# Elementwise steps of three token mixers moved from GpSimd to VectorE in a two-layer hybrid decoder step

## The chip, the cores and the metric

The kernel runs on one core of a Trainium2 chip. The metric is the device time of one execution of the whole program, in microseconds. A core has TensorE (PE: matmuls and transposes; PEld is its weight load), VectorE (DVE), ScalarE (ACT), GpSimd (POOL) and SyncE (SP, which issues the DMAs here). Each engine runs its own queue of instructions in the order in which the program gives them, and engines wait for each other by semaphores.

## What is computed

Two trunk layers over 1104 tokens (16 learned meta tokens, 1024 prompt tokens, 8 sequences of 8 decode tokens). In each layer three mixers read one input projection: a gated delta rule (4 heads, key and value width 128), a Mamba2 scan (4 heads of 64, state 128) and sliding-window attention with rotary positions. Their outputs are joined and projected, and a SwiGLU block follows.

```
(dn_qkv, dn_z, dn_b, dn_a, ssm_xbc, ssm_z, ssm_dt, sw_q, sw_k, sw_v) = split_cols(h @ lw['w_in'], IN_WIDTHS)
a_mat = where(strict, beta_i * (k_i . k_j) * decay_ij, 0);  attn = (q_i . k_j) * decay_ij     # delta rule
o_c = q_dec @ s + attn @ v_new;  s = s * g_last + k_dec^T v_new
attn = (c_i . b_j) * decay_ij;  y_intra = attn @ (x * dt);  h = h * g_last + xdt^T b_dec       # scan
rope(x) = [x1*cos - x2*sin, x2*cos + x1*sin]                                                  # attention
x = x + rmsnorm(mixed @ w_out);  x = x + rmsnorm((silu(gate) * up) @ w_ffn_out)
```

## The kernel before

Matmuls of weights run in pairs of half-precision values (a high and a low part, three products each); the small matmuls of the mixers run in fp32. Tokens are cut into nine tiles, eight of 128 and one of 80 (the 64 decode tokens and the last 16 of the prompt), and the delta rule works on quads of tiles (4, 4, 1) per head.

The program is not written in its final order. Every step is a generator (`dense`, `swa_in`, `ssm_pre`, `ssm_seq`, `dn_inv`, `dn_prep`, `dn_chain` and others), and class `Plan` picks, again and again, the first generator by priority whose data is ready on the planner's own clock of TensorE. For that it keeps a clock per engine: an elementwise instruction of n elements per partition is costed at `RATE[engine][0] * n + RATE[engine][1]` ns.

```
RATE = {"V": (1.04, 90.0), "S": (0.85, 55.0), "G": (2.1, 60.0)}
```

V is VectorE, S ScalarE, G GpSimd; the power function on GpSimd has a surcharge. So the engine that an instruction is given to alters the order of everything around it, on all engines. `conv_post` (the convolutions, tiles `u` and `R`) and the weight splitting (`wsp`) add VectorE work when the planner's VectorE clock is free.

The steps that the change touches, with their lines:
- `rope_tile` (660): per token tile four products of the projected q and k (`qkv`) with sines and cosines into `rp`, and one sum. It runs right after each of the first nine projections of a layer.
- `lt_make` (1482) and `ssm_pre` (1847): per tile of the scan, the decay matrix `lt` times the causal mask, and x times three scalings (`xdt`, `xde`, `xD`). VectorE then multiplies `lt` with a product of TensorE, and TensorE reads `lt`, `xdt` and `xde`.
- `dn_inv` (1543) and `dn_prep` (1651): per quad the decay matrix `M` times the mask and times beta; per tile `qe` (in `prep`) times q.
- `dn_chain` (1683), for a head's last tile: spread values `ye` and the eight decode states `Sb` times their decay. VectorE writes `r` and `S` of the chain; `ps_ch` is the one PSUM bank of the chain.
- `ssm_seq` (1897), last tile: `xe` and the decode states `hs`, as in `dn_chain`.

GpSimd also computes every inverse square root (`rsqrt`, line 572: `rqy`, one multiply-add and one power), diagonals (`affine_select`), fills, and small copies (`coll`). All engine calls go through one wrapper, so every instruction's line is L215, and rows are told apart by tiles.

Of the kernel before, what the change touches and what calls it, by code (L numbers as in the profile page):

```python
# [284 lines left out]
def build(tc, A, depth=DEPTH):  # L285
# [3 lines left out]
    V, S, G, T, DQ = (P.engine(e, k) for e, k in ((nc.vector, "V"), (nc.scalar, "S"), (nc.gpsimd, "G"),  # L289
                                                 (nc.tensor, "T"), (nc.sync, "D")))  # L290
# [26 lines left out]
    MUL, ADD, SUB, MAX = ALU.mult, ALU.add, ALU.subtract, ALU.max  # L317
# [342 lines left out]
    def rope_tile(qkv, i, C, L):  # L660
        cs, sn = (L.KSW(n)[:C, i * 64:i * 64 + 64] for n in ("cs", "sn"))
        x = qkv[:C, :384].rearrange("p (h e d) -> p h e d", e=2, d=32)
        t1, t2 = (abp.tile([128, 6, 2, 32], F32, tag="a", name="rp")[:C] for _ in range(2))
        snv = sn.rearrange("p (e d) -> p e d", e=2)
        csv = cs.rearrange("p (e d) -> p e d", e=2)
        for e in range(2):
            G.tensor_tensor(t2[:, :, e, :], x[:, :, 1 - e, :],
                            snv[:, e:e + 1, :].to_broadcast([C, 6, 32]), op=MUL)
            G.tensor_tensor(t1[:, :, e, :], x[:, :, e, :],
                            csv[:, e:e + 1, :].to_broadcast([C, 6, 32]), op=MUL)  # L670
        G.tensor_tensor(qkv[:C, :384], t1.rearrange("p h e d -> p (h e d)"),
                        t2.rearrange("p h e d -> p (h e d)"), op=ADD)

    def put_mixed(mx, c0, n, ps, p0=0, pn=128, view=None):
# [807 lines left out]
    def lt_make(lt, p, L, ths, C):  # L1482

        n = len(ths)
        for k, (i, h) in enumerate(ths):
            act(lt[:, k], p[:C, k, :C], AF.Relu, bias=L.gc[:C, i, h:h + 1], scale=-1.0)
        act(lt, lt, AF.Exp, scale=-1.0)
        mk = U[:, None, :] if C == 128 else U8[:80, None, :]
        G.tensor_tensor(lt, lt, mk.to_broadcast([C, n, C]), op=MUL)


    QUADS = ((0, 1, 2, 3), (4, 5, 6, 7), (8,))
# [2 lines left out]
    def col(X, i):  # L1495
        return X["c"] if i == 8 else X["u"][:, i * 128:i * 128 + 128]
# [46 lines left out]
    def dn_inv(L, w, it):  # L1543
# [6 lines left out]
        for h, b in it:  # L1550
            H = L.HS[h]
            C, n = tsz(b[0]), len(b)
            yield (("gates", l),)
            yield "inv"
            p = v4(PS("inv"))
            for k, i in enumerate(b):
                T.transpose(p[:, k, :C], gc[:C, i, h:h + 1].to_broadcast([C, 128]), ident[:C, :C])
            M = t4("M")[:C, :n, :C]
# [2 lines left out]
            yield None  # L1561
            act(M, M, AF.Exp, scale=-1.0)
            mk = U[:, None, :] if C == 128 else U8[:80, None, :]
            G.tensor_tensor(M, M, mk.to_broadcast([C, n, C]), op=MUL)
            yield None
            yield (("q", l, h), ("k", l, h))
            G.tensor_tensor(M, M, H["b2"][:C, b[0]:b[0] + n].unsqueeze(2).to_broadcast([C, n, C]), op=MUL)
            yield None
            yield lambda: outst[0] < 3
            outst[0] += 1  # L1570
# [80 lines left out]
    def dn_prep(L):  # L1651

        l, gc = L.l, L.gc
        for h in range(4):
            H = L.HS[h]
            for b in PAIRS:
                C, n = tsz(b[0]), len(b)
                yield (("q", l, h), ("k", l, h), ("v", l, h), ("sk", l, h), ("gates", l))
                yield lambda: outst[1] < 2
                outst[1] += 1  # L1660
                X = big([128, 4, 2, 128], F32, "prep")
                qe, kd, vt = X[:, 0], X[:, 1], X[:, 2]
                yield "tr"
                p = v4(PS("tr"))
                for k, i in enumerate(b):
                    T.transpose(p[:, k, :C], gc[:C, i, h:h + 1].to_broadcast([C, 128]), ident[:C, :C])
                act(qe[:, :n, :C], p[:, :n, :C], AF.Exp)
                for k, i in enumerate(b):
                    G.tensor_tensor(qe[:, k, :C], qe[:, k, :C], col(H["q"], i), op=MUL)
                yield NOW  # L1670
                yield "tr"
                p = v4(PS("tr"))
                for k, i in enumerate(b):
                    T.transpose(p[:C, k, :], col(H["k"], i), ident)
                    T.transpose(p[:C, 2 + k, :], col(H["v"], i), ident)
                for k, i in enumerate(b):
                    act(kd[:C, k], p[:C, k], scale=H["d2"][:C, i:i + 1])
                    act(vt[:C, k], p[:C, 2 + k], scale=H["sk"][:C, i:i + 1])
                    H["X"][i] = (qe[:, k], kd[:, k], vt[:, k])
                mark(("prep", l, h, b[0]))  # L1680
                yield None

    def dn_chain(L):
# [3 lines left out]
        nE, gl, gls = L.nE, L.gl, L.gls  # L1687
        for h in range(4):
            H = L.HS[h]
            Sst = dnp.tile([128, 128], F32, tag="S", bufs=2, name="S")  # L1690
            V.memset(Sst, 0.0)
            for qd, b in enumerate(QUADS):
                og = None
                C = tsz(b[0])
                for k, i in enumerate(b):
# [3 lines left out]
                    qe, kd, vt = H["X"].pop(i)  # L1699
                    if i == 5:  # L1700
                        Sb = big([128, 8, 128], F32, "Sb")
                        dma(Sb, A["Sb"][l, h])
                    if C != 128:
                        kq = big([128, 8, 128], F32, "kq")
                        G.memset(kq, 0.0)
                        for src, o in ((H["k"]["c"][:, 0:64], 0), (qe[:, 0:64], 64)):
                            d = bass.AP(kq.tensor, kq.offset + o, [list(kq.ap[0]), [136, 8], [1, 8]])
# [58 lines left out]
                if C != 128:  # L1766
                    mark(("S", l, h))
                    later(("S", l, h), lambda h=h, Sst=Sst: dma(A["dn_p"][l, h], Sst))
                    ye = big([128, 4, 128], F32, "ye")
                    for q in range(2):  # L1770
                        o = slice(q * 32, q * 32 + 32)
                        G.tensor_tensor(ye[o], y[o].unsqueeze(1).to_broadcast([32, 4, 128]),
                                        SEGM[o, 4 * q:4 * q + 4].unsqueeze(2).to_broadcast([32, 4, 128]), op=MUL)
                    G.tensor_tensor(Sb, Sb, gls[:, 0:8, h:h + 1].to_broadcast([128, 8, 128]), op=MUL)
                    P.add(1, dn_last(L, h, Sb, ye, kd))

    def dn_last(L, h, Sb, ye, kd):
# [69 lines left out]
    def ssm_pre(L, it):  # L1847
# [6 lines left out]
        for i in it:  # L1854
            C = tsz(i)
# [14 lines left out]
            act(xk[:C], px[:C])  # L1870
            x4 = xk[:C, 0:256].rearrange("p (h d) -> p h d", h=4)
            xdt, xde, xD = r2("xdt", 2), r2("xde", 3), r2("xD", 3)
            G.tensor_tensor(xdt[:C], x4, L.dt[:C, i, :].unsqueeze(2).to_broadcast([C, 4, 64]), op=MUL)
            G.tensor_tensor(xde[:C], x4, L.xdd[:C, i, :].unsqueeze(2).to_broadcast([C, 4, 64]), op=MUL)
            G.tensor_tensor(xD[:C], x4, vec[:C, 20:24].unsqueeze(2).to_broadcast([C, 4, 64]), op=MUL)
            zt = r2("zt", 3)
            yield ((("zt", l, i), "st"),)
            dma(zt[:C].rearrange("p h d -> p (h d)"), zd[l, i * 128:i * 128 + C, :])
# [18 lines left out]
    def ssm_seq(L):  # L1897
# [10 lines left out]
        for i in range(NT):  # L1908
            C = tsz(i)
# [56 lines left out]
            if i == 8:  # L1966
                mark(("hT", l))
                later(("hT", l), lambda: dma(A["ssm_p"][l], h2))
                for g in range(2):
                    xe = big([128, 4, 128], F32, "xe")  # L1970
                    for q in range(2):
                        o = slice(q * 32, q * 32 + 32)
                        G.tensor_tensor(xe[o], xde[o, 2 * g:2 * g + 2].rearrange("p h d -> p (h d)").unsqueeze(1)
                                        .to_broadcast([32, 4, 128]),
                                        SEGM[o, 4 * q:4 * q + 4].unsqueeze(2).to_broadcast([32, 4, 128]), op=MUL)
                    for r_ in range(2):
                        hv = hs[g][:, :, r_ * 64:r_ * 64 + 64]
                        G.tensor_tensor(hv, hv, gls[:, 0:8, 4 + 2 * g + r_:5 + 2 * g + r_]
                                        .to_broadcast([128, 8, 64]), op=MUL)
                    yield None  # L1980
                    pq = []
# [308 lines left out]
```

## Time and profile before

| | us |
|---|---|
| median of 3 runs (2830.35 to 2835.38) | 2833.14 |
| the profiled execution | 2830.23 |
| its span, first to last instruction | 2828.4 |
| TensorE busy | 2719.1 |
| VectorE busy | 2011.9 |
| GpSimd busy | 494.7 |

The profile comes from one execution. Stages follow each other in time in each layer: projections and attention, the scan, the delta rule, the output projection, SwiGLU. TensorE's projections for a later stage fill the time of an earlier one, so a stage is read from the trace by the tiles that are worked on: in the first layer the rotations lie at 35 to 112 us, the scan at 225 to 320 us and the delta rule at 320 to 665 us; in the second at 1440 to 1500, 1627 to 1721 and 1721 to 2066 us.

### The profile page before, as it was taken

To read this page: it belongs to the slowest core of one execution; us is meant where nothing else is said; L and a number is where in the kernel's file an instruction comes from. 1 tells how busy PE (TensorE), PEld (TensorE's weight loads), DVE (VectorE), ACT (ScalarE), POOL (GpSimd) and SP (SyncE) were. 2 spreads that over 40 slices of the span, in tenths; PEclk is the share of its full clock that TensorE was granted. 3 is DMA by queue.
4 is the path that set the end of the run, shared out by engine and by line. 5 is a ranking of instruction groups with operands and counts; after the bars stand their busy time and mean duration, and the time that the engine had idled before them with its cause. 6 is when DMAs were issued, how large, how long until landed. Compare 5 with 4: busy or idle time off the path is not lost. (4 is left out here: it accounts for less than half of the span.)

```text
span 2828.4 us, 49806 instructions
## 1 busy us (share of the span) xinstructions
PE 2719.1 (96%) x19662; PEld 1900.6 (67%) x19662; DVE 2011.9 (71%) x3992; ACT 1281.4 (45%) x3015; POOL 494.7 (17%) x746
## 2 busy tenths in 40 slices
PE   7999998999899999999999989999998999999998
PEld 4767676765688888744458666777646888886443
DVE  6467667655867777868875776676569677777778
ACT  5445456654433333433544455556544333334343
POOL 3205423312200000000260063233122000000002
PEclk9999999999999999999999999999999999999999
DMA  5011100132311111342340111001232111113424
GB/s 196 29 64 47 49 31 32 39 105 92 111 39 52 60 46 57 102 119 97 124 151 19 66 49 42 29 32 52 93 113 89 46 60 47 61 53 105 117 100 150
DMA packets 74092, 209.78 MB, mean 74 GB/s; under 512 B 13361, under 2 KB 24817, under 8 KB 73825
## 3 DMA queue, kind: packets, MB, share of 16 engines
q1 hardware_dynamic: 73856, 206.59, 22.1%
q8 instruction: 154, 2.52, 0.4%
q14 instruction: 82, 0.66, 0.1%
HBM read 175.49 MB, written 33.04 MB: 74 GB/s over the span
## 5 line engine op out<-in xcount | busy, mean ns | idle before, releaser
L215 PEld LDWEIGHTS <-wsp 128*128 128x128 f16 x10704 | 1041.7, 98 | 304.7 <-issue 13.6
L215 PE MATMUL pd<-xn,wsp 128*128 128x336 f16 (+3 forms) x4512 | 737.0, 311 | 2.3 <-DVE m L215 2.1
L215 ACT ACTIVATE wsp<-raw 128x512 f16<-128x512 f32 (+2 forms) x390 | 286.5, 751 | 398.9 <-DVE raw L215 70.6
L215 DVE SCALAR_TENSOR_TENSOR wsp<-raw,wsp 128x512 f16<-128x512 f32 (+2 forms) x390 | 326.8, 848 | 66.2 <-ACT wsp L215 63.4
L215 PEld LDWEIGHTS <-hsp 128*128 128x128 f16 x1848 | 181.0, 98 | 222.0 <-DVE hsp L215 3.5
L215 POOL TENSOR_SCALAR rqy<-ss 128x1 f32<-128x1 f32 (+1 forms) x72 | 69.6, 967 | 1445.6 <-ACT jk L215 1235.4
L215 PE MATMUL pd<-wsp,hsp 128*128 128x512 f16 x924 | 224.1, 381 | 3.4 <-DVE hsp L215 1.7
L215 PE MATMUL ps_o<-wsp,hsp 128*128 128x512 f16 x924 | 222.4, 379 | 0.1
L215 PE MATMUL pd<-wsp,mixed 128*128 128x512 f16 (+1 forms) x864 | 210.3, 381 | 0.0
L215 DVE SCALAR_TENSOR_TENSOR u<-R,lp_cw,u 128x512 f32<-128x512 f32 x216 | 179.6, 866 | 11.3 <-ACT u L215 10.4
L215 ACT ACTIVATE hsp<-hid 128x512 f16<-128x512 f32 x154 | 89.7, 619 | 183.0 <-PE ps_o L215 157.6
L215 PE MATMUL ps_o<-xn,wsp 128*128 128x256 f16 (+1 forms) x1296 | 161.3, 281 | 0.0
L215 PE MATMUL pd<-wsp,xn 128*128 128x512 f16 (+3 forms) x864 | 156.2, 332 | 3.2 <-ACT wsp L215 1.7
L215 PE MATMUL ps_inv<-xn,wsp 128*128 128x256 f16 (+1 forms) x1248 | 154.1, 281 | 0.0
L215 PEld LDWEIGHTS <-mixed 128*128 128x128 f16 (+1 forms) x864 | 84.0, 101 | 75.6 <-issue 4.5
L215 DVE TENSOR_TENSOR hsp<-hid,hsp 128x512 f16<-128x512 f32 x154 | 101.0, 683 | 41.7 <-ACT hsp L215 41.7
L215 PEld LDWEIGHTS <-xn 128*128 128x128 f16 (+1 forms) x864 | 86.2, 101 | 50.9 <-issue 3.1
L215 PE MATMUL ps_ch<-xn,wsp 128*128 128x296 f16 x456 | 109.2, 289 | 0.0
L215 PE MATMUL ps_tr<-xn,wsp 128*128 128x256 f16 x456 | 108.6, 273 | 0.0
L215 DVE TENSOR_TENSOR raw<-raw 128x512 f32<-128x512 f32 x152 | 103.9, 686 | 2.3 <-DMA raw<-wfi 0.8
L215 DVE TENSOR_TENSOR W<-ps_inv,c 128x512 f16<-128x512 f32 (+1 forms) x120 | 71.0, 595 | 47.3 <-PE ps_inv L215 46.4
L215 ACT ACTIVATE R<-pd 128x384 f32<-128x384 f32 (+3 forms) x180 | 56.2, 359 | 81.9 <-PE pd L215 81.5
(490 smaller groups left out, 4602.4 us busy)
## 6 DMA issues: line engine op xcount, KB each, us to landing
raw<-wfi SPq DMA_DIRECT2D x88, 512.0 KB, 3.5
raw<-wfo SPq DMA_DIRECT2D x50, 512.0 KB, 3.7
raw<-wf SPq DMA_DIRECT2D x44, 512.0 KB, 3.3
xd<-xt SPq DMA_DIRECT2D x24, 512.0 KB, 2.9
xt<-xd SPq DMA_DIRECT2D x24, 512.0 KB, 4.6
rawg<-wfo SPq DMA_DIRECT2D x20, 512.0 KB, 4.3
xt<-x SPq DMA_DIRECT2D x16, 512.0 KB, 4.9
raw<-wo SPq DMA_DIRECT2D x16, 512.0 KB, 3.4
```

Of the source, the lines that this page charges most:

```text
L215: r = f(*a, **kw)
```

## The change

Fourteen calls in seven functions name another engine: `G` becomes `V`. Nothing else is edited. GpSimd keeps the powers, the fills, the diagonal selection and the small copies.

```diff
@@ rope_tile
         for e in range(2):
-            G.tensor_tensor(t2[:, :, e, :], x[:, :, 1 - e, :],
+            V.tensor_tensor(t2[:, :, e, :], x[:, :, 1 - e, :],
                             snv[:, e:e + 1, :].to_broadcast([C, 6, 32]), op=MUL)
...
-        G.tensor_tensor(qkv[:C, :384], t1.rearrange("p h e d -> p (h e d)"),
+        V.tensor_tensor(qkv[:C, :384], t1.rearrange("p h e d -> p (h e d)"),
@@ lt_make
-        G.tensor_tensor(lt, lt, mk.to_broadcast([C, n, C]), op=MUL)
+        V.tensor_tensor(lt, lt, mk.to_broadcast([C, n, C]), op=MUL)
@@ dn_inv
-            G.tensor_tensor(M, M, mk.to_broadcast([C, n, C]), op=MUL)
+            V.tensor_tensor(M, M, mk.to_broadcast([C, n, C]), op=MUL)
...
-            G.tensor_tensor(M, M, H["b2"][:C, b[0]:b[0] + n].unsqueeze(2).to_broadcast([C, n, C]), op=MUL)
+            V.tensor_tensor(M, M, H["b2"][:C, b[0]:b[0] + n].unsqueeze(2).to_broadcast([C, n, C]), op=MUL)
@@ dn_prep
-                    G.tensor_tensor(qe[:, k, :C], qe[:, k, :C], col(H["q"], i), op=MUL)
+                    V.tensor_tensor(qe[:, k, :C], qe[:, k, :C], col(H["q"], i), op=MUL)
@@ dn_chain
-                        G.tensor_tensor(ye[o], y[o].unsqueeze(1).to_broadcast([32, 4, 128]),
+                        V.tensor_tensor(ye[o], y[o].unsqueeze(1).to_broadcast([32, 4, 128]),
...
-                    G.tensor_tensor(Sb, Sb, gls[:, 0:8, h:h + 1].to_broadcast([128, 8, 128]), op=MUL)
+                    V.tensor_tensor(Sb, Sb, gls[:, 0:8, h:h + 1].to_broadcast([128, 8, 128]), op=MUL)
@@ ssm_pre
-            G.tensor_tensor(xdt[:C], x4, L.dt[:C, i, :].unsqueeze(2).to_broadcast([C, 4, 64]), op=MUL)
+            V.tensor_tensor(xdt[:C], x4, L.dt[:C, i, :].unsqueeze(2).to_broadcast([C, 4, 64]), op=MUL)
...
@@ ssm_seq
-                        G.tensor_tensor(xe[o], xde[o, 2 * g:2 * g + 2].rearrange("p h d -> p (h d)").unsqueeze(1)
+                        V.tensor_tensor(xe[o], xde[o, 2 * g:2 * g + 2].rearrange("p h d -> p (h d)").unsqueeze(1)
...
-                        G.tensor_tensor(hv, hv, gls[:, 0:8, 4 + 2 * g + r_:5 + 2 * g + r_]
+                        V.tensor_tensor(hv, hv, gls[:, 0:8, 4 + 2 * g + r_:5 + 2 * g + r_]
```

Since the planner costs the instructions anew, the order changes on every engine. Three places of VectorE's queue show how; in all of them `u<-R` and `u<-t` are convolution work and `wsp` a weight's low part.

**A. The scan, first layer, near its middle.** VectorE before, from one tile's `y` to the `lt` that TensorE reads next:

```order
L215 TENSOR_TENSOR y_2667<-y_2667,rqy 128x256
L215 SCALAR_TENSOR_TENSOR u<-R,lp_cw,u 128x616
L215 SCALAR_TENSOR_TENSOR mixed<-ps_tr,nwy,mixed 128x128
L215 TENSOR_TENSOR y_2837<-ps_inv,E 128x256
L215 TENSOR_TENSOR hT<-hT,ps_o 128x256
L215 TENSOR_TENSOR lt<-ps_inv,lt 128x2x128 x2
```

The same part of VectorE's queue after the change:

```order
L215 TENSOR_TENSOR lt<-lt,c_87 128x512
L215 TENSOR_TENSOR xdt<-xk,s_1553 128x256
L215 TENSOR_TENSOR xde<-xk,xdd 128x256
L215 TENSOR_TENSOR xD<-xk,lp_vec 128x256
L215 SCALAR_TENSOR_TENSOR mixed<-ps_tr,nwy,mixed 128x128
L215 TENSOR_TENSOR lt<-ps_inv,lt 128x2x128 x2
L215 SCALAR_TENSOR_TENSOR mixed<-ps_tr,nwy,mixed 128x128
L215 TENSOR_TENSOR y_2817<-y_2817,rqy 128x256
L215 SCALAR_TENSOR_TENSOR u<-R,lp_cw,u 128x512
```

The four scalings of a tile now stand ahead of the product `lt<-ps_inv,lt`, and the convolution work stands behind it.

**B. The last tile of the second delta-rule head, first layer.** VectorE before, up to the `r` of the decode rows, which the chain on TensorE needs:

```order
L215 TENSOR_TENSOR on<-ps_o,rqy 128x256
L215 SCALAR_TENSOR_TENSOR u<-R,lp_cw,u 128x616
L215 SCALAR_TENSOR_TENSOR u<-R,lp_cw,u 128x512
L215 SCALAR_TENSOR_TENSOR u<-R,lp_cw,u 128x616
L215 SCALAR_TENSOR_TENSOR r<-ps_ch,nE,prep 64x128
```

GpSimd before at this place:

```order
L215 TENSOR_SCALAR rqy<-sso 128x4
L215 TENSOR_TENSOR rqy<-rqy,mhalf 128x4
L215 TENSOR_TENSOR Sb<-Sb,gls 128x1024
```

VectorE after:

```order
L215 TENSOR_TENSOR on<-ps_o,rqy 128x256
L215 SCALAR_TENSOR_TENSOR r<-ps_ch,nE,prep 64x128
L215 TENSOR_TENSOR W<-ps_inv,c_88 128x512
L215 TENSOR_TENSOR Sb<-Sb,gls 128x1024
L215 TENSOR_TENSOR M<-ps_inv,M 128x512
L215 SCALAR_TENSOR_TENSOR r<-ps_ch,nE,prep 16x128
```

`Sb` now stands behind the first `r` on the same engine, and the convolutions no longer stand between `on` and `r`; `on`, which takes a power from GpSimd, still stands ahead of `r`.

**C. The start, first layer.** VectorE after the change, where the last two norms of the input (`xt`, 128 and 80 rows) stood next to each other before:

```order
L215 SCALAR_TENSOR_TENSOR xt<-xt,rqy,gb_100 128x1024
L215 TENSOR_TENSOR rp<-qkv,csb 128x6x32
L215 TENSOR_TENSOR rp<-qkv,csa 128x6x32
L215 TENSOR_TENSOR rp<-qkv,csb 128x6x32
L215 TENSOR_TENSOR rp<-qkv,csa 128x6x32
L215 SCALAR_TENSOR_TENSOR xt<-xt,rqy,gb_100 80x1024
L215 TENSOR_TENSOR qkv<-rp 128x384
```

The first tile's rotation now stands between the two norms. The number of DMAs on SP's queue is unchanged; a few stand earlier or later among each other.

## Rows read from the trace of the kernel before

**Rows 1.** Page, parts 1 and 2: busy us of each engine; VectorE, GpSimd and TensorE clock by slice.

```profile
PE 2719.1 (96%) x19662; PEld 1900.6 (67%) x19662; DVE 2011.9 (71%) x3992; ACT 1281.4 (45%) x3015; POOL 494.7 (17%) x746
...
POOL 3205423312200000000260063233122000000002
PEclk9999999999999999999999999999999999999999
```

**Rows 2.** Busy time by stretch: window, length, then PE, PEld, DVE, ACT, POOL, granted clock, DMA.

```profile
35.00:112.00 77.00, 75.01 (x515) 49.76 (x514) 50.82 (x101) 40.41 (x124) 33.22 (x50) 0.96 0.13 42
225.00:320.00 95.00, 85.91 (x616) 65.38 (x615) 67.79 (x143) 47.46 (x132) 56.56 (x75) 0.96 0.13 43
320.00:665.00 345.00, 328.77 (x2610) 237.49 (x2608) 217.46 (x471) 198.06 (x526) 92.09 (x149) 0.99 0.15 51
849.00:919.00 70.00, 70.00 (x598) 58.30 (x596) 54.26 (x129) 24.61 (x56) 0.00 (x0) 1.00 0.15 52
1627.00:1721.00 94.00, 85.86 (x617) 65.50 (x616) 67.51 (x143) 47.37 (x132) 57.15 (x75) 0.96 0.14 44
1721.00:2066.00 345.00, 328.83 (x2611) 237.29 (x2609) 218.29 (x472) 198.06 (x526) 92.73 (x151) 1.00 0.15 51
```

**Rows 3.** What TensorE waited for, 225 to 320 us: total, times, longest.

```profile
PE ps_ch L215 <- DVE lt L215: 3.9, 2, 2.0
PE ps_tr L215 <- DVE mixed L215: 2.8, 2, 2.4
PE ps_ch L215 <- POOL xde L215: 0.9, 1, 0.9
```

**Rows 4.** The same, 320 to 665 us.

```profile
PE ps_ch L215 <- ACT qs L215: 6.7, 3, 3.2
```

**Rows 5.** Timeline at 490 us: start, us, engine, tiles, [idle before, releaser].

```profile
489.94 1.91 POOL L215 TENSOR_TENSOR Sb<-Sb,gls 128x1024 f32<-128x1024 f32 x1
489.98 0.42 DVE L215 TENSOR_TENSOR on<-ps_o,rqy 128x256 f32<-128x256 f32 x1 [1.20 <-POOL rqy L215]
...
490.32 3.62 DVE L215 SCALAR_TENSOR_TENSOR u<-R,lp_cw,u 128x616 f32<-128x616 f32 x3
493.87 0.33 DVE L215 SCALAR_TENSOR_TENSOR r<-ps_ch,nE,prep 64x128 f32<-64x128 f32 x1
...
494.56 0.61 PE L215 MATMUL ps_ch<-S,ck 128*16 128x128 f32 x2 [3.21 <-ACT qs L215]
```

**Rows 6.** Busy time by stretch, columns as in rows 2.

```profile
305.00:313.00 8.00, 8.00 (x36) 4.89 (x35) 1.94 (x9) 0.99 (x5) 0.96 (x2) 0.57 0.03 12
493.00:500.00 7.00, 5.44 (x27) 3.52 (x28) 3.22 (x8) 3.20 (x7) 1.34 (x2) 0.52 0.00 0
```

**Rows 7.** VectorE groups, 130 to 225 us: xcount | busy, mean ns | idle before.

```profile
L215 DVE SCALAR_TENSOR_TENSOR u<-R,lp_cw,u 128x616 f32<-128x616 f32 x18 | 15.4, 853 | 0.0
```

**Rows 8.** VectorE groups, 225 to 320 us.

```profile
L215 DVE SCALAR_TENSOR_TENSOR u<-R,lp_cw,u 128x616 f32<-128x616 f32 x9 | 11.5, 1281 | 0.0
...
L215 DVE TENSOR_TENSOR lt<-ps_inv,lt 128x256 f32<-128x256 f32 x16 | 6.0, 411 | 5.8 <-PE ps_inv L215 5.8
L215 DVE TENSOR_TENSOR y<-y,rqy 128x256 f32<-128x256 f32 x8 | 5.3, 658 | 6.1 <-POOL rqy L215 6.1
```

**Rows 9.** GpSimd groups, 225 to 320 us.

```profile
L215 POOL TENSOR_TENSOR lt<-lt,c 128x512 f32<-128x512 f32 x8 | 11.4, 1425 | 0.0
L215 POOL TENSOR_TENSOR xD<-xk,lp_vec 128x256 f32<-128x256 f32 x8 | 7.5, 937 | 0.0
```

**Rows 10.** VectorE groups of the whole span, all operands in SBUF.

```profile
L215 DVE TENSOR_TENSOR raw<-raw 128x512 f32<-128x512 f32 x152 | 103.9, 686 | 2.3 <-DMA raw<-wfi 0.8
...
L215 DVE TENSOR_TENSOR m<-m,gpo 128x1024 f32<-128x1024 f32 x16 | 19.5, 1219 | 3.9 <-ACT xn L215 3.9
...
L215 DVE TENSOR_TENSOR hid<-U,hid 128x256 f32<-128x256 f32 x76 | 28.5, 416 | 0.0
...
L215 DVE TENSOR_TENSOR on<-on,rqy 80x128 f32<-80x128 f32 x8 | 2.3, 285 | 5.1 <-issue 4.9
```

More of the change, by code (lines that the diff above doesn't have):

```diff
@@ L666, in rope_tile @@
         for e in range(2):
-            G.tensor_tensor(t2[:, :, e, :], x[:, :, 1 - e, :],
+            V.tensor_tensor(t2[:, :, e, :], x[:, :, 1 - e, :],
                             snv[:, e:e + 1, :].to_broadcast([C, 6, 32]), op=MUL)
-            G.tensor_tensor(t1[:, :, e, :], x[:, :, e, :],
+            V.tensor_tensor(t1[:, :, e, :], x[:, :, e, :],
                             csv[:, e:e + 1, :].to_broadcast([C, 6, 32]), op=MUL)
-        G.tensor_tensor(qkv[:C, :384], t1.rearrange("p h e d -> p (h e d)"),
+        V.tensor_tensor(qkv[:C, :384], t1.rearrange("p h e d -> p (h e d)"),
                         t2.rearrange("p h e d -> p (h e d)"), op=ADD)
@@ L1872, in ssm_pre @@
             xdt, xde, xD = r2("xdt", 2), r2("xde", 3), r2("xD", 3)
-            G.tensor_tensor(xdt[:C], x4, L.dt[:C, i, :].unsqueeze(2).to_broadcast([C, 4, 64]), op=MUL)
-            G.tensor_tensor(xde[:C], x4, L.xdd[:C, i, :].unsqueeze(2).to_broadcast([C, 4, 64]), op=MUL)
-            G.tensor_tensor(xD[:C], x4, vec[:C, 20:24].unsqueeze(2).to_broadcast([C, 4, 64]), op=MUL)
+            V.tensor_tensor(xdt[:C], x4, L.dt[:C, i, :].unsqueeze(2).to_broadcast([C, 4, 64]), op=MUL)
+            V.tensor_tensor(xde[:C], x4, L.xdd[:C, i, :].unsqueeze(2).to_broadcast([C, 4, 64]), op=MUL)
+            V.tensor_tensor(xD[:C], x4, vec[:C, 20:24].unsqueeze(2).to_broadcast([C, 4, 64]), op=MUL)
             zt = r2("zt", 3)
```

## The prediction, made before the changed kernel ran

> **What bounds the kernel now.** I begin with the page's busy times [rows 1]: TensorE works 2719.1 of 2828.4 us, so all idle time together is 109.3 us, and no change on another engine can give back more than that and what the clock loses. VectorE is at 71%, GpSimd at 17%, and GpSimd's slices show where it works: at the start of each layer and in the mixers, never in SwiGLU. So only the mixer stretches can change. The table by stretch [rows 2] tells how full they are. In SwiGLU (849 to 919 us) TensorE is busy all the time. In the scan of the first layer it is idle 95 - 85.9 = 9.1 us, in the delta rule 345 - 328.8 = 16.2 us; the second layer repeats this (8.1 and 16.2 us). That is 49.6 us of idle time. The same rows give the granted clock: 0.96 over the scans is (1 - 0.96) x 95 = 3.8 us lost in each layer, 0.99 over the first delta rule about 3.4 us, 11 us in all. The reader is to see that about 60 us is the whole prize, in stretches where VectorE is busy 71% (scan) and 63% (delta rule).
>
> Next come the waits of TensorE. In the scan it waits for VectorE's `lt` and `mixed` and for GpSimd's `xde`, 7.6 of the 9.1 us [rows 3]; in the delta rule the largest item is 6.7 us for ScalarE's `qs` [rows 4]. The timeline at 490 us [rows 5] shows what lies behind the longest of these. GpSimd starts `Sb` at 489.94 and holds it 1.91 us. VectorE, which had been idle 1.20 us for a power from GpSimd, starts three convolution steps at 490.32, and they take 3.62 us, where their kind without GpSimd takes 853 ns for 616 elements [rows 7]. The chain's `r` stands behind them, `qs` behind `r`, and TensorE idles 3.21 us. Right after such a gap the clock is down: 0.52 from 493 to 500 us, and 0.57 from 305 to 313 us after the scan's gap of 2.4 us [rows 6], against 1.00 elsewhere. 0.5 is the lower of the two levels (1.2 of 2.4 GHz), so the first of these costs 0.48 x 7 = 3.4 us and the second the same.
>
> The slowdown is general: the same convolution step takes 853 ns where GpSimd hardly works [rows 7] and 1281 ns in the scan; `y` times its norm, which reads two SBUF operands, takes 658 ns there, while `lt<-ps_inv,lt` of the same 256 elements, with one operand in PSUM, keeps its 411 ns [rows 8]. A VectorE instruction that reads two tensors from SBUF waits for a GpSimd instruction that reads SBUF.
>
> **The change, part by part.** By the loops it moves 322 instructions in two layers: 90 of the rotations, 18 masks of `lt`, 54 scalings of x, 48 on `M`, 72 on `prep`, 16 `ye`, 8 `Sb`, 8 `xe`, 8 `hs`.
>
> Price on VectorE, from groups with all operands in SBUF [rows 10]: 686 ns for 512 elements, 1219 for 1024, 416 for 256, 285 for 128; on the line between them 550 for 384, 350 for 192, 235 for 80 and 500 for 320. The sum: 80 of 512 (16 `lt`, 32 `M`, 16 `ye`, 8 `xe`, 8 `hs`) 54.9 us; 8 of 1024 9.8; 18 of 384 9.9; 54 of 256 22.5; 72 of 192 25.2; 64 of 128 18.2; 24 of 80 and two of 320 6.6. Together 147 us. Broadcast operands have no row of their own at these sizes; from below they cannot cost less than a row of the same length, from above GpSimd's 1425 and 937 ns [rows 9] are a far bound. I take the rows of VectorE.
>
> Against it stands what VectorE no longer waits for. In one scan the 616-element steps give back 9 x 0.43 = 3.9 us and `y` 8 x 0.24 = 1.9 [rows 7, 8]; with the other two-operand groups I estimate 10 us. The price in that stretch is 9 `lt` (6.0), 27 scalings (11.2), and `xe` and `hs` (5.5), 22.7 us. So VectorE goes there from 67.8 to about 80 of 95 us, 85%. In the delta rule the price is 33 us (16 + 8 on `M`, 36 on `prep`, 8 `ye`, 4 `Sb`) and the relief I estimate at 5, so 217 becomes 245 of 345, 71%. In the rotations 36 x 0.35 + 9 x 0.55 = 17.6 us make 50.8 into at most 68 of 77.
>
> None of this lies on TensorE, whose instructions stay the same in number. It matters only where TensorE waits. Why should it wait less while VectorE has more to do? Because the gaps are places where the chip runs behind the planner's clocks, and the order is fixed by those clocks. The planner costs 616 elements on VectorE at 1.04 x 616 + 90 = 731 ns and a mask of 512 on GpSimd at 2.1 x 512 + 60 = 1135; the scan shows 1281 and 1425. A scaling of 256 is costed 598 on GpSimd and shows 937 [rows 8, 9]. In one scan that is 9 x 0.55 + 8 x 0.29 + 8 x 0.34 = 10 us that nobody planned for, in these three groups alone. On VectorE the same work is costed 622 (512) and 356 (256) and should take 686 and 416, and the step 853: 9 x 0.12 + 8 x 0.06 + 8 x 0.06 = 2 us. The extra load itself is in the plan: place A of the order shows the four scalings ahead of `lt` with the convolutions put behind it.
>
> Term 1, the scans: idle 17.2 and clock 7.6 us, 24.8 together. Nothing at all and all of it are the bounds; I take half, **-12.4 us**, since unplanned time falls by more than that share while the load rises.
>
> Term 2, the delta rule: the long gap at 490 us goes from 3.2 to about 1.7, because at place B `r` stands right behind `on`, which still waits for a power (1.20 us idle now). In two layers 3.0 us, with the first layer's clock 3.4 us, and 1.6 us from the other two gaps behind `qs` (6.7 - 3.2 = 3.5 us together in a layer) [rows 4], of which I take 0.8 us off one in each layer. **-8 us**; bounds 0 and the 13.4 us of `qs` (6.7 in each layer) and 3.4 of clock.
>
> Term 3, new lateness from a fuller VectorE: below 0 is excluded, since work is only added there; above, all of the net load, 147 less some 30 of relief. By the nearest rows the gaps of the delta rule that have nothing to do with GpSimd (16.2 less 6.7 us) exist at 63% load; from there to 71% I allow a third more, 3 us a layer. **+6 us**. The rotations I cost at nothing: TensorE is busy 75.0 of 77 us there [rows 2], covered by projections that are ready. Without that cover it would be the 17 us a layer of their price.
>
> GpSimd's own queue gets shorter, so the powers start sooner; that is in term 2's and term 1's shares. SP's queue issues the same DMAs, and no wait in rows 3 and 4 is for one. ScalarE's instructions stay.
>
> Sum: 2830.2 - 12.4 - 8 + 6 = 2815.8 on the profiled execution. The median of the runs stands 2.9 us above that execution, so I expect a median of about **2818 us**.
>
> **The rivals.**
> *TensorE's gaps only change places.* A new order has new gaps where the plan is wrong about ScalarE, powers and chains. For it: the waits for `on`, `at`, `r`, `S` and `qs` don't come from GpSimd's sharing alone. The gain of term 2's clock and a part of term 1 is eaten: 2829 us, within 0.2% (5.7 us, about what a measurement of this kernel can tell from no change).
>
> *VectorE becomes the bound of the scan.* A tile of the scan takes 95 / 9 = 10.6 us, and VectorE would work about 8.9 us of them, with chains that leave it idle in between. From the point where its work for a tile, with the waits for powers, passes 10.6 us, `lt` comes late on every tile, and TensorE waits behind `ps_ch`. Price: idle and clock of the scans double, +25, term 2 is halved to -4, and a clock drop more at each start, +3.4 x 2, makes +28 at worst; at half of that 2846 us. Against it: convolution work can be put off, as place A shows. The Trainium skill (Perfetto Trace Analysis, Optimizing Scalar/DVE Operations) says that with a saturated VectorE, moving work to GpSimd may make sense, though sharing a read port the two may not gain. By that rule this change goes the wrong way once VectorE is full; the trace has it at 71% in the scan, and shows the sharing itself at 1281 against 853 ns.
>
> *All of it comes back.* Gaps behind GpSimd vanish with their clock losses: -25 and -15, about 2796 us with nothing lost to load.
>
> *The change doesn't do what it says* is excluded by the order: all 322 instructions stand on VectorE.
>
> **How the numbers follow.** Forecast 0.44, the larger gain 0.13, places changed 0.20, VectorE the bound 0.23. Faster 0.57, same 0.20, slower 0.23. The forecast's own range is 2806 to 2827. For 8 in 10 I go down to 2798, which leaves out the best cases, and up to 2846, which takes in half of the slow case.
>
> **What would show it.** Right: the 616-element steps at about 853 ns in the scan; VectorE at 2012 + 147 - 30 to 50, some 2120 us; GpSimd well under 300 us; the wait for `lt` under 2 us and the clock at 1.00 in both scans; no gap over 2 us for `qs`. Wrong: if `ps_ch <- DVE lt` grows in the scan or TensorE shows new waits for VectorE at the start of a layer, term 3 was too small; if the waits at tile 8 stay near 3 us, the power was their cause and not `Sb`.

## The result: 38 us faster, and the profile after

| | before | changed |
|---|---|---|
| median, us | 2831.74 (4 runs, 2828.20 to 2835.38) | 2793.57 (4 runs, 2791.98 to 2795.64) |
| ratio, 95% interval | | 0.9871 [0.9859, 0.9884] |
| span of the profiled execution | 2828.4 | 2792.4 |

The direction was the one forecast; the size was not: 38 us instead of 14, below the range (2798 to 2846). The page of the changed kernel, parts 1 and 2, for [rows 1]:

```profile
PE 2711.8 (97%) x19662; PEld 1902.3 (68%) x19662; DVE 2081.6 (75%) x4314; ACT 1274.5 (46%) x3015; POOL 236.1 (8%) x424
...
POOL 1001111011200000000210011111021000000002
PEclk9999999999999999999999999999999999999999
```

TensorE's idle time, span less busy, went from 109.3 to 80.6 us (-28.7). Its busy time fell by 7.3 us with the same 19662 matmuls. The mean granted clock is 0.990 in both executions, so this is not the clock; the ends of matmuls are modelled, so the likely place is stalls shorter than a matmul, which count as busy. Together 36.0 us, the difference of the spans. VectorE does 322 instructions more and is busy 69.7 us longer.

The table by stretch, for [rows 2]: window, length, then PE, PEld, DVE, ACT, POOL, granted clock, DMA. Rotations, scan, delta rule of the first layer, scan and delta rule of the second:

```profile
35.00:112.00 77.00, 74.95 (x512) 50.55 (x511) 58.17 (x143) 39.38 (x123) 0.98 (x4) 0.96 0.14 43
225.00:320.00 95.00, 92.93 (x676) 70.22 (x675) 79.01 (x190) 51.47 (x145) 16.30 (x37) 0.98 0.16 54
320.00:645.00 325.00, 316.13 (x2543) 231.61 (x2542) 234.04 (x540) 191.82 (x514) 38.04 (x71) 0.99 0.16 51
1608.00:1700.00 92.00, 90.73 (x652) 68.83 (x651) 75.34 (x182) 50.24 (x140) 15.22 (x33) 0.96 0.15 50
1700.00:2029.00 329.00, 319.35 (x2569) 232.90 (x2568) 238.25 (x549) 192.83 (x519) 39.03 (x75) 0.99 0.16 52
```

Idle time of TensorE in the two scans: 2.1 + 1.3 = 3.3 us, from 17.2. In the two delta rules: 8.9 + 9.6 = 18.5, from 32.4. So 27.8 of the 28.7 us are in these four stretches, 13.9 in each kind. In the first scan TensorE does 676 matmuls in the 95 us in which it did 616. (The second window is shorter than before, 325 and 329 us for 345, because the delta rule ends sooner.) The clock is hardly better: (1 - 0.98) x 95 + (1 - 0.96) x 92 = 5.6 us lost in the scans, from 7.6.

TensorE's waits, 225 to 320 us, for [rows 3], total, times, longest:

```profile
PE ps_tr L215 <- DVE mixed L215: 1.4, 2, 0.8
PE ps_inv L215 <- DVE lt L215: 0.6, 1, 0.6
```

and 320 to 645 us, for [rows 4]:

```profile
PE ps_tr L215 <- DVE on L215: 1.9, 2, 1.3
PE ps_inv L215 <- DVE T L215: 1.4, 1, 1.4
PE ps_ch L215 <- DVE S L215: 1.0, 2, 0.9
...
PE ps_ch L215 <- ACT qs L215: 0.4, 1, 0.4
```

The waits behind `ps_ch` for `lt`, 3.9 us, are gone, with 0.6 us left behind `ps_inv`; the 6.7 us for `qs` became 0.4, and no gap in these two stretches is over 1.4 us. VectorE's groups in the scan, for [rows 7, 8], show the price of the moved steps (`lt<-lt,c`, `xde`) and what the others gained: xcount | busy us, mean ns | idle before:

```profile
L215 DVE SCALAR_TENSOR_TENSOR u<-R,lp_cw,u 128x616 f32<-128x616 f32 x11 | 9.3, 850 | 0.0
...
L215 DVE TENSOR_TENSOR lt<-ps_inv,lt 128x256 f32<-128x256 f32 x16 | 6.0, 413 | 0.0
L215 DVE TENSOR_TENSOR lt<-lt,c 128x512 f32<-128x512 f32 x8 | 5.5, 685 | 0.2 <-ACT lt L215 0.2
...
L215 DVE TENSOR_TENSOR y<-y,rqy 128x256 f32<-128x256 f32 x8 | 3.3, 418 | 1.8 <-POOL rqy L215 1.8
...
L215 DVE TENSOR_TENSOR xde<-xk,xdd 128x256 f32<-128x256 f32 x8 | 3.3, 418 | 0.0
```

The convolution step is at 850 ns instead of 1281, `y<-y,rqy` at 418 instead of 658, and `lt<-ps_inv,lt`, with an operand in PSUM, keeps its 413.

### The profile page after: what moved, and what is told of

Read it like the earlier page. It is cut to its first block, busy times and chain, and to the rows that moved or that the text cites. A ratio compares the mean times of both kernels' runs of the same rounds, so it can differ in the third digit from the quotient of the medians.

```text
span 2792.4 us, 49684 instructions
## 1 busy us (share of the span) xinstructions
PE 2711.8 (97%) x19662; PEld 1902.3 (68%) x19662; DVE 2081.6 (75%) x4314; ACT 1274.5 (46%) x3015; POOL 236.1 (8%) x424
## 5 line engine op out<-in xcount | busy, mean ns | idle before, releaser
L215 DVE SCALAR_TENSOR_TENSOR wsp<-raw,wsp 128x512 f16<-128x512 f32 (+2 forms) x390 | 322.6, 837 | 64.0 <-ACT wsp L215 60.4
L215 DVE SCALAR_TENSOR_TENSOR u<-R,lp_cw,u 128x512 f32<-128x512 f32 x216 | 165.6, 797 | 8.6 <-ACT u L215 8.5
```

The source lines that it names most:

```text
L215: r = f(*a, **kw)
```

## The experiments

Eighteen kernels ran, each timed in five rounds beside the kernel before. Ratios are to that kernel; a change of 0.001 is 2.8 us.

### Order or durations

The move does two things: the instructions take other times, and the planner writes another order. Two kernels separate them.

```diff
+    GV = P.engine(nc.vector, "G")      # order_kept: planned as GpSimd's, run on VectorE
-        V.tensor_tensor(...)           # all fourteen calls
+        GV.tensor_tensor(...)
```

> All 322 instructions run on VectorE, but are planned as GpSimd's, so that the order of the program stays that of the kernel before. Theory A (the chip ran behind the plan, because GpSimd's steps and the VectorE steps beside them took longer than planned): most of the 38 us is here without a new order, 2796 to 2806 us; the 616-element steps near 850 ns in the scan. Theory B (the new order is what gains): 2824 us or more, since VectorE gets 147 us that no one planned for. Between 2806 and 2824 both have a share.

Measured: 2792.79 us, 0.9862 [0.9849, 0.9875]. The whole gain, in nearly the old order: compared line by line in the traces, with tile numbers left out, TensorE's 19662 instructions differ from those of the kernel before in 720 lines and from those of the changed kernel in 5296.

```diff
+    VG = P.engine(nc.gpsimd, "V")      # order_alone: planned as VectorE's, run on GpSimd
-        V.tensor_tensor(...)
+        VG.tensor_tensor(...)
```

> The reverse: the order of the changed kernel, with the 322 instructions run on GpSimd. Theory A: the plan is now more wrong than before (a mask of 512 is planned at 622 ns and takes 1425), so 2830 to 2860 us. Theory B: the order brings the gain with it, 2795 to 2812 us.

Measured: 2831.36 us, 1.0002 [0.9993, 1.0011]. The order without the move is worth nothing. Theory B falls. One row of this run bears on the prediction's second term, TensorE's wait for `qs` from 320 to 670 us:

```profile
PE ps_ch L215 <- ACT qs L215: 2.0, 1, 2.0
```

Here GpSimd has all of its old work, and of the 6.7 us for `qs` in the kernel before most is gone all the same, with no gain in time. So the new order alone shortens this wait, and that by itself gains nothing.

### Which part

Three kernels move only some of the fourteen calls, and a fourth all but the rotations'.

```diff
-        G.tensor_tensor(lt, ...), (xdt, ...), (xde, ...), (xD, ...), (xe, ...), (hs, ...)
+        V.tensor_tensor                # scan_part
-        G.tensor_tensor(M, ...) twice, (qe, ...), (ye, ...), (Sb, ...)
+        V.tensor_tensor                # delta_part
-        G.tensor_tensor(t2, ...), (t1, ...), (qkv, ...)
+        V.tensor_tensor                # rot_part
```

> Only the scan's instructions move (lt, xdt, xde, xD, xe, hs: 88 of 322). The traces put about 15 us of lost idle time and some 3 us of smaller stalls in the scans. Theory A: each stretch gains by itself, 2811 to 2817 us. Rival C (the gain comes from the port and not from the place: it needs GpSimd quiet everywhere): under a third of the gain, 2820 us or more. If the order of the layer as a whole counts, less in the scans and changes in the delta rule.

> Only the delta rule's instructions move (both on M, prep, ye, Sb: 144 of 322). The traces put about 14 us of idle time there. Theory A: 2814 to 2820 us, and together with the scan's part the whole 38 us. Rival C: under a third, 2822 us or more; then the parts sum to less than the whole.

> Only the rotations' 90 instructions move. The scan's part alone gave -19.7 us and the delta rule's -7.9, which leaves 10 of the 38 us. If parts simply add, the rotations are worth those 10 us: 2821 us. If the 10 us need scan and delta rule together (work that GpSimd shares over stretches), the rotations give nothing, as the prediction had it: 2828 to 2834 us.

> Scan and delta rule moved, the rotations left on GpSimd. Alone the parts gave -19.7, -7.9 and, for the rotations, 0; the whole -38. If scan and delta rule need each other (GpSimd quiet over the whole mixer, or gaps that only change places when one part alone is cured): 2792 to 2798 us. If the rotations count once the rest is gone: about 2804 us.

| | median, us | ratio | TensorE idle, us |
|---|---|---|---|
| scan_part | 2811.78 | 0.9927 [0.9914, 0.9940] | 92.5 |
| delta_part | 2823.60 | 0.9973 [0.9962, 0.9983] | 101.7 |
| rot_part | 2830.35 | 1.0001 [0.9992, 1.0010] | 110.4 |
| scan_delta | 2790.93 | 0.9853 [0.9840, 0.9867] | 81.3 |

The scan is about half of the gain, as the idle times of the stretches said. The rotations are worth nothing. Scan and delta rule alone give 20.7 and 7.6 us by the ratios, together 41.6, some 13 us more than the sum. Rival C, that GpSimd must be quiet everywhere, is wrong for the scan; for the delta rule its forecast (2822 us or more, and parts that sum to less than the whole) came true. But each of these kernels is planned anew, and further down the order alone moves a kernel with a quiet GpSimd by up to 32 us. So it is not shown that the 13 us need both parts; they may be luck of the orders. The mean granted clock was 0.987 in delta_part against 0.990 before and 0.993 in scan_delta, so a part of the 13 us lies in the clock; how much was not settled.

### What in GpSimd's work costs

The changed kernel gets the old load back on GpSimd, for nobody. Each ghost is a multiplication (or a run of fills) that adds nothing to the output.

```diff
+    def ghost(like):                   # called behind each moved instruction, same shape
+            nc.gpsimd.tensor_tensor(gh[:c, :w], c32[:c, :w], c32[:c, :w], op=ALU.mult)   # ghost
+            nc.gpsimd.memset(gh[:c, :min(256, n - o)], 0.0)      # ghost_fill, 3 n elements
```

> The changed kernel, and GpSimd does a multiplication of the same shape beside each moved instruction, on constants, for nobody. VectorE keeps all the work, and no step waits for GpSimd's copy. Theory A1 (what costs is that VectorE's two-operand instructions and the powers stand beside or behind GpSimd's long steps): most of the gain goes back, 2820 us or more; the 616-element steps of the scan rise again towards 1281 ns. Theory A2 (the moved steps are simply shorter on VectorE, 0.7 instead of 1.4 us, and that is what the chains gain): the gain stays, 2793 to 2803 us.

> As the run before, but GpSimd fills a scratch tile with zeros for about as long instead of multiplying; it reads nothing from SBUF. Theory A1 with the read of SBUF as its cause: 616-element steps at about 850 ns and 2793 to 2803 us. Theory A3 (the powers wait in GpSimd's queue behind long steps, whatever these do): as much is lost as with the multiplications. Theory A2: 2793 to 2803 us, so that this run and the one before tell A1 from A2 and A3 together.

Measured: 2954.73 us, 1.0437 [1.0422, 1.0451], and 2915.39, 1.0296 [1.0282, 1.0310]. Both are far above any expectation, and the reason is on the first run's page: GpSimd's slices, busy tenths in 40 slices.

```profile
POOL 8896011111021000000022001111113000000002
```

The ghosts wait for nothing, and the build put them at the start of the program, where the first norms wait for GpSimd: in the first 290 us VectorE's `xt` waits 142 us for the power `rqy`. These two runs answer nothing about the mixers. They gave one number: a ghost multiplication of 512 elements takes 1084 ns there. In the next two each ghost is held behind the GpSimd instruction ahead of it in program order, and the rotations have none.

```diff
-            nc.gpsimd.tensor_tensor(gh...)
+            tc.keep_in_program_order(nc.gpsimd.tensor_tensor(gh...))    # ghost_pin
-            nc.gpsimd.memset(gh...)
+            tc.keep_in_program_order(nc.gpsimd.memset(gh...))           # ghost_fill_pin, 2 n elements
```

> The ghost of the earlier run, held in its place: each of GpSimd's multiplications on constants stands behind the instruction that GpSimd has before it in program order, and only the 232 instructions of scan and delta rule have one (the rotations' part was worth nothing). VectorE does all the work; nothing waits for the copies. Theory A1 (neighbours suffer: VectorE's two-operand steps are slowed and the powers queue up): 2815 us or more, 616-element steps of the scan well above 850 ns. Theory A2 (the moved steps are shorter on VectorE, that is all): 2793 to 2803 us. With the run of fills beside it the slowing is told from the queue.

> The same, with GpSimd filling a scratch tile with zeros for about as long at the same places, so that it reads nothing. Theory A3 (powers stand behind long steps in GpSimd's queue): as much lost as with the multiplications. Theory A1 by slowed VectorE steps: these keep about 850 ns and the loss is under a third of that with the multiplications. Theory A2: 2793 to 2803 us.

Measured: 2829.10 us, 0.9991 [0.9982, 1.0000], and 2793.38 us, 0.9870 [0.9852, 0.9889]. Multiplications that read SBUF take the whole gain away; fills take nothing, with nearly the same load on GpSimd. (The fills are cut into pieces of 256 elements, 311 ns each, so that four of them stand for one multiplication of 512.) The page, part 1, of ghost_pin:

```profile
PE 2723.1 (96%) x19662; PEld 1904.4 (67%) x19662; DVE 2135.0 (76%) x4314; ACT 1276.2 (45%) x3015; POOL 460.0 (16%) x664
```

and of ghost_fill_pin:

```profile
PE 2710.4 (97%) x19662; PEld 1900.7 (68%) x19662; DVE 2082.8 (75%) x4314; ACT 1274.4 (46%) x3015; POOL 414.4 (15%) x1010
```

GpSimd is busy 460 and 414 us, so its queue is about as full in both; VectorE is busy 52 us longer in the first, with the same 4314 instructions. Its groups in the scan, 225 to 320 us, of ghost_pin:

```profile
L215 DVE SCALAR_TENSOR_TENSOR u<-R,lp_cw,u 128x616 f32<-128x616 f32 x11 | 12.4, 1127 | 0.0
...
L215 DVE TENSOR_TENSOR lt<-ps_inv,lt 128x256 f32<-128x256 f32 x16 | 5.9, 409 | 0.0
...
L215 DVE TENSOR_TENSOR y<-y,rqy 128x256 f32<-128x256 f32 x7 | 3.7, 534 | 2.5 <-POOL rqy L215 2.5
```

and of ghost_fill_pin:

```profile
L215 DVE SCALAR_TENSOR_TENSOR u<-R,lp_cw,u 128x616 f32<-128x616 f32 x11 | 9.4, 851 | 0.0
...
L215 DVE TENSOR_TENSOR lt<-ps_inv,lt 128x256 f32<-128x256 f32 x16 | 6.0, 411 | 0.0
...
L215 DVE TENSOR_TENSOR y<-y,rqy 128x256 f32<-128x256 f32 x8 | 3.3, 417 | 2.1 <-POOL rqy L215 2.1
```

The wait for the power `rqy` is nearly the same in both, 2.5 and 2.1 us. So the difference between these two runs is not the queue (A3) and, since the moved steps run on VectorE in both, not their own shorter time (A2): what costs here is that VectorE's instructions with two SBUF operands are slowed while GpSimd reads SBUF. The Trainium skill (SBUF — State Buffer, Who interferes with whom) states just this, that a VectorE instruction with two SBUF inputs contends with a GpSimd instruction that reads SBUF, "not with one that only writes it"; these two runs agree, with 1127 and 851 ns. Two things must be kept in mind. In ghost_pin VectorE has the moved work and the slowing, in the kernel before only the slowing. And in the kernel before `y` waits 6.1 us for the power in this stretch [rows 8], which neither run brings back. So the pair shows that the slowing is enough to cost the whole gain; how the 38 us divide between the slowing, the powers' place in GpSimd's queue and the moved steps' own length is not shown. For the last the trace of the kernel before gives a hint: over the whole span the waits of TensorE's matmuls that end with a moved step are the two below (its weight loads have 8.2 us more), and VectorE has none.

```profile
PE ps_ch L215 <- POOL xde L215: 1.9, 2, 1.0
PE ps_tr L215 <- POOL ye L215: 0.5, 2, 0.2
```

### What a fuller VectorE costs

The changed kernel, with VectorE doing the moved instructions of one stage a second time, on constants.

```diff
+            tc.keep_in_program_order(nc.vector.tensor_tensor(gh..., op=ALU.mult))
+    ghost(M), ghost(M), ghost(qe), ghost(ye), ghost(Sb)                       # vload_delta
+    ghost(lt), ghost(xdt), ghost(xde), ghost(xD), ghost(xe), ghost(hv)        # vload_scan
```

> The changed kernel, and VectorE does each moved instruction of the delta rule a second time, on constants and for nobody, unplanned: about 34 us more in each layer's delta rule (234 to about 268 of 325 us, 82%), with GpSimd as quiet as in the changed kernel. If load below the full engine is free, as the changed kernel suggests: 2793 to 2800 us. By my third term (3 us a layer for 8% more load): about 2799 to 2803. If every extra instruction in a chain's way delays it: up to the 68 us, 2810 us or more.

> The same for the scan's instructions: about 22.7 us more a layer, where the changed kernel has VectorE at 79 of 95 us, so that it would be asked for 102. My second rival (VectorE becomes the bound of the scan) must bite here if anywhere: at least 7 us a layer, 2807 us or more. If convolution steps can be put off into the delta rule even then: 2793 to 2803 us.

Measured: 2812.40 us, 0.9933 [0.9921, 0.9946], and 2822.87 us, 0.9963 [0.9951, 0.9976]. This load, on top of what the change brings, is not free. VectorE's busy time rose by 50.3 us (2131.9 on the page) in the first and by 34.8 (2116.4) in the second, and the time by 18.8 and 29.3 us: 0.4 and 0.8 us for each. (The profiled execution of the second is the fastest of its five, 2814.84 us; by its span the figure is 0.6.) In vload_scan the stretch of the scan (the last multiplication of `hs` ends at 332.2 us instead of 322.6) reads, columns as above:

```profile
225.00:330.00 105.00, 96.54 (x688) 71.31 (x686) 96.29 (x232) 53.95 (x146) 21.93 (x37) 0.96 0.15 49
```

VectorE is busy 92% of it, TensorE idles 8.5 us. That is my second rival, at the load where it bites. In ghost_pin the same stretch has VectorE nearly as full, 88%, without the second copy of the work, by the slowing:

```profile
225.00:333.00 108.00, 100.82 (x690) 74.22 (x689) 94.89 (x196) 53.47 (x147) 58.77 (x75) 0.94 0.14 48
```

### The planner's price, and luck

By the durations in the profile VectorE's instructions take 1.04 ns an element and 150 ns, where the planner says 90. The prediction had blamed the gaps on such differences.

```diff
-    RATE = {"V": (1.04, 90.0), "S": (0.85, 55.0), "G": (2.1, 60.0)}
+    RATE = {"V": (1.04, 150.0), "S": (0.85, 55.0), "G": (2.1, 60.0)}     # rate_fix, before_150
+    RATE = {"V": (1.04, 120.0), "S": (0.85, 55.0), "G": (2.1, 60.0)}     # rate_120, before_120
```

> The changed kernel, planned with VectorE's measured price: 1.04 ns an element and 150 ns instead of 90 (which gives 682, 416 and 283 ns for 512, 256 and 128 elements; the profile has 685, 418 and 283). My prediction held the gaps to be places where the chip runs behind the planner's clocks. If that is so, part of the 80.6 us that TensorE still idles goes: 2775 to 2788 us. If order matters as little as the two runs on it showed: 2788 to 2799 us.

> The changed kernel planned with 120 ns instead of 90 for VectorE's fixed part; 150, the measured value, cost 22 us. If a truer plan is by itself worse (work is placed later than it needs to be): between the two, 2798 to 2812 us. If each new order is a draw with a spread of that size: anywhere from 2785 to 2820 us. If 150 was an outlier: within 4 us of 2793.

> The kernel before, planned with 120 ns instead of 90 for VectorE's fixed part; the changed kernel came to 2783.4 us with it. If the move is worth its 38 us in any order: 2815 to 2830 us here, some 38 above that. If the measured gain was mostly a lucky order: under 2800 us.

> The same with 150 ns, where the changed kernel came to 2815.9 us. If the move is worth some 38 us in any order: 2840 to 2865 us. If an order is a draw by itself, unconnected with that of the changed kernel: 2815 to 2850 us. If the gain was mostly luck: under 2820 us.

| planned fixed part, ns | kernel before, us | changed kernel, us | difference |
|---|---|---|---|
| 90 | 2831.74 | 2793.57 | 38 |
| 120 | 2830.58, 1.0001 [0.9992, 1.0010] | 2783.38, 0.9834 [0.9818, 0.9850] | 47 |
| 150 | 2826.15, 0.9979 [0.9970, 0.9988] | 2815.86, 0.9943 [0.9930, 0.9955] | 10 |

The price that fits the durations is no better order: 22 us worse at 150, 10 better at 120. Both results lie outside every range that was expected of them, and for the kernel before only "a draw by itself" holds at 150. One reason may be that 150 isn't the truer price: neighbours share 57 ns on VectorE (worked out below), so what an instruction adds to its busy time is nearer 150 - 57 = 93 ns, an estimate, and the planner's 90 was close to that.

And the order matters after all once GpSimd is quiet: the changed kernel spreads over 32 us, the kernel before over 6. The loss at 150 ns has several places. TensorE's idle time is 94.3 us in rate_fix and 78.4 in rate_120, and its busy time 16.5 us longer with the same matmuls; the mean granted clock is 0.985 against 0.992, which over the spans is 42 against 22 us lost. The first delta rule (to 645 us) and, in the second layer, the scan and the delta rule, of rate_fix:

```profile
337.00:645.00 308.00, 294.29 (x2408) 221.46 (x2406) 215.69 (x503) 183.37 (x497) 33.32 (x66) 0.98 0.15 51
1600.00:1735.00 135.00, 129.80 (x903) 95.83 (x901) 104.24 (x244) 68.62 (x178) 21.88 (x46) 0.95 0.15 50
1735.00:2075.00 340.00, 325.28 (x2531) 236.57 (x2530) 234.39 (x523) 193.94 (x512) 39.18 (x76) 0.97 0.18 61
```

and of rate_120:

```profile
337.00:645.00 308.00, 300.64 (x2452) 221.47 (x2451) 222.03 (x517) 186.20 (x504) 33.85 (x70) 0.99 0.17 55
1600.00:1735.00 135.00, 134.83 (x988) 100.70 (x986) 113.57 (x261) 73.99 (x195) 21.38 (x48) 0.99 0.15 50
1735.00:2075.00 340.00, 328.64 (x2533) 229.69 (x2531) 241.83 (x526) 199.51 (x517) 42.80 (x80) 1.00 0.20 65
```

TensorE idles 13.7, 5.2 and 14.7 us in these windows, against 7.4, 0.2 and 11.4. Only the first layer's scan is near empty of gaps in both (0.9 and 0.1 us from 227 to 337 us). So the sign of the gain is the same at all three prices, its size is not, and a part of the 38 us may be luck. The three differences average 32 us. rate_120 is the fastest version found, 10 us below the changed kernel.

### One step further

```diff
-        G.tensor_scalar(y, x, mul, add, op0=MUL, op1=ADD)
+        V.tensor_scalar(y, x, mul, add, op0=MUL, op1=ADD)      # rsqrt; madd_on_v, and on scan_delta
```

> One step further than the change: the multiply-add ahead of each power of minus one half (122 instructions in the trace, 0.2 to 0.95 us each on GpSimd) runs on VectorE too. If short links in the chains of norms still hold TensorE up (the gaps behind on and y in the changed kernel), each power comes up to 0.7 us sooner: 2783 to 2790 us. If the hop between the engines costs as much as it saves, or the chains are no longer on the path: 2790 to 2797 us.

> Scan and delta rule on VectorE, rotations left on GpSimd, and the multiply-add ahead of the powers on VectorE. Alone the first gave 2790.9 and the second, with the whole change, 2795.8, against 2793.6 for the change. If shorter chains of norms still help: 2780 to 2788 us. If they don't, as that run says: 2788 to 2796 us.

Measured: 2795.77 us, 0.9874 [0.9859, 0.9889], and 2803.35 us, 0.9899 [0.9885, 0.9912]. The step took 114 instructions to VectorE by the traces, not the 122 expected. No gain, and in the second a loss of 12 us, which is within the spread of orders; these runs can't tell a loss of the step from one of its order.

## Why the prediction was wrong, step by step

The sum was -14.4 us and the spans differ by 36.0. Taken apart, the terms forecast 8.6 us less idle time in the scans (half of 17.2), 1.4 us more in the delta rules (4.6 less by term 2, 6 more by term 3) and 7.2 us from the clock (3.8 and 3.4). The profiles have 13.9 us less in the scans, 13.9 less in the delta rules, 0.9 less elsewhere, nothing from the clock over the span, and 7.3 us less busy time, for which there was no term. The step that failed most is the delta rule: its gain was made too small and then more than cancelled by a charge for a fuller VectorE, whose cost did not show there.

**The prize and its place: right.** "About 60 us" in the mixers; 27.8 us of idle time went there, and SwiGLU and the rotations gave nothing.

**The mechanism: half right.** The slowing of VectorE's two-operand instructions was read from the right rows [rows 7, 8], and the two held ghosts show that it is enough to cost the whole gain. But I made it an argument about planning ("the gaps are places where the chip runs behind the planner's clocks"), and there the runs went against me: prices that fit the durations better don't help, and order_kept gains all 38 us although its 147 us of work on VectorE are planned on GpSimd's clock and not on VectorE's.

**Term 1, -12.4 us: mis-sized.** Half of the scans' idle and clock was taken. Idle fell by 13.9 of 17.2 us and the clock's loss by 2.0, 15.9 together, and the scan's part alone measured 20.7 us. The two things that I named as its causes, slowed steps and long GpSimd steps, were removed whole, and nothing in the rows spoke for keeping half of their cost: my own figure for the unplanned time falls by four fifths, from 10 to 2 us.

**Term 2, -8 us: mis-sized, and its reason was wrong.** Idle fell by 13.9, of which 12.6 behind `qs` (6.7 to 0.4 us in each layer). The gap at 490 us did not shrink by a half but went. I had kept half of it for the power that `on` waits for. That wait is still there, and `r` follows it at once, but TensorE has other work meanwhile:

```profile
483.52 0.42 DVE L215 TENSOR_TENSOR on<-ps_o,rqy 128x256 f32<-128x256 f32 x1 [1.21 <-POOL rqy L215]
...
484.03 0.34 DVE L215 SCALAR_TENSOR_TENSOR r<-ps_ch,nE,prep 64x128 f32<-64x128 f32 x1
```

Nor is this wait what the gain is made of: it is 2.0 us in order_alone and 1.3 in ghost_pin (320 to 670 us), and both are as slow as the kernel before. The 3.4 us that I hoped for from the clock did not come, as the stretches still read 0.99. Moved alone, the delta rule's part gave 7.6 us, and planned at 150 ns much of its gain is lost.

**Term 3, +6 us: not there.** In the delta rule VectorE came to 234 of 325 us, 72%, as worked out (71%), but the gaps that have nothing to do with `qs` did not grow by a third: from 19.0 us in two layers (32.4 less 13.4) they went to 17.7 (18.5 less 0.8). Load on top of that does cost, 0.4 to 0.8 us for a microsecond of VectorE's time in the two runs above; from the load of the change itself no such cost shows there. Over the whole span the load was also estimated too high. VectorE was to reach 2120 us and reached 2081.6. The price of 147 us was right to the microsecond (the moved groups sum to 146.8), and the relief of "30 to 50" too: the other groups sum to 50.3 us less. What I missed is that neighbours overlap: summed over all groups the records of before come to 2240.3 us and busy is 2011.9, so each of 3992 instructions shares 57 ns with the next. After the change 26.8 us more are such overlap (2336.8 - 2081.6, less 2240.3 - 2011.9). The Trainium skill (Perfetto Trace Analysis, Optimizing Scalar/DVE Operations) says it: VectorE's overhead on SBUF is about 60 ns, and a profiled duration holds about twice that, half of it beside the next instruction. By that rule the price is 147 less 322 x 0.06 = 128 us, an estimate; the trace comes near it, with 120 (146.8 - 26.8) if all of the added overlap is put down to the moved steps.

**The rivals.** "All of it comes back", 2796 us, was nearest and had a chance of 0.13. By its own terms it is lower: 2830.2 - 25 - 15 and the 2.9 us of the median make 2793, and 2793.57 was measured. That they meet is in part luck: its price was right for the delta rule (13.9 for 15) and high for the scans (15.9 for 25), and 7.3 us of busy time that no term had came on top. "VectorE becomes the bound of the scan" did not come: VectorE is at 79 of 95 us, as worked out. That it is a real limit is shown by vload_scan. The rule of the Trainium skill (Perfetto Trace Analysis, Optimizing Scalar/DVE Operations), that with a saturated VectorE work may go to GpSimd, is not tested by this change: VectorE was at 71% in the scan and went to 83%. "Gaps only change places" describes rate_fix better than the change.

**The tests named:** convolution steps at 853 ns (850), GpSimd well under 300 us (236.1), `lt` under 2 us (0.6), no `qs` gap over 2 us (0.4) came out. The clock at 1.00 in both scans did not (0.98 and 0.96), nor did VectorE at some 2120 us (2081.6).

**The range.** 2798 left out the best case on the ground that some loss to load was likely. Both runs of added load show such losses, so the ground was fair, though the change itself shows none in the delta rule; the width wasn't. An order that a planner draws anew can differ by 32 us on the same instructions, and a range that knows nothing of that is too narrow.

## What to carry to other kernels

Before an elementwise step is given to GpSimd to spare VectorE, count the VectorE instructions beside it that read two SBUF operands: here GpSimd's elementwise steps kept it busy 259 us longer, the durations of VectorE's other instructions summed to 50 us more, and taking these steps to VectorE made the kernel 38 us faster, a part of which may be luck of the order. Fills cost nothing of the kind in this kernel. Where a planner writes the order, run a change at two or three planner prices before its size is believed.

## What the runs showed that was not expected

- GpSimd's fills, for about as long as the multiplications in sum, leave VectorE alone (851 ns a step, 2793.4 us); the multiplications don't (1127 ns, 2829.1 us).
- GpSimd's own steps are longer too where VectorE works beside them: the same ghost multiplication of 512 elements takes 1084 ns in ghost, where all of them stand in the first 290 us and VectorE is busy 121 of these, and 1240 on average in ghost_pin, inside the mixers. That VectorE is the reason is likely, not shown.
- The granted clock gave nearly nothing back: both kernels have a mean of 0.990 over the span, though TensorE idles 28.7 us less. I had booked the clock's loss behind each gap as part of that gap.
- With GpSimd busy the kernel hardly reacts to the planner's price (6 us), with GpSimd quiet it does (32 us). At 150 ns a large part of the loss goes with the granted clock (0.985 for 0.992 at 120). Why the order matters only then is open.
